# Down projection of a hybrid decoder trunk: loads of two Strassen operands placed behind the next chunk's, norm products moved into the second group's pairs, order at the end pinned

## The chip, the cores and the metric

The kernel runs on one core of one Trainium2 chip. The metric is the device time of one execution in microseconds (us), lower is better; a kernel is run three times and the median is given. A profile is one further execution, taken by the hardware profiler; its span runs from the first to the last recorded instruction, and the execution's own time is a little longer than its span.

## The reference

One decoder layer over 256 tokens of width 2048, with 16 meta tokens ahead, all in float32. Heads of differential attention and of chunkwise retention share one input projection and one output projection; then come a gated MLP with a causal convolution and a final RMS norm. Cut to what matters here:

```python
def conv_glu(u, w_gate, w_up, conv_w, w_down):
    g = u @ w_gate
    ...
    return (jax.nn.silu(gc) * (u @ w_up)) @ w_down          # 256x5632 @ 5632x2048

def reference(x, ...):
    ...
        h = h + y @ w_out[l]
        u = rmsnorm(h, ffn_norm[l]) * vmask
        h = h + conv_glu(u, w_gate[l], w_up[l], conv_w[l], w_down[l])

    out = rmsnorm(h, final_norm)
    return out[:, CHUNK:]
```

The change is in the product with `w_down` and in the final norm. Everything ahead of them stays as it was.

## The kernel before, in words

**Arithmetic.** TensorE multiplies a rounded form of float32. So each operand is split into a high half (ScalarE casts it, L223) and a low half (VectorE subtracts the cast from the original, L224), and each product is three matmuls, high by high, high by low and low by high (`triple`, L888 to L890). Weights come from DRAM in chunks, are split by `prep`, and are read by TensorE from the tiles `whi` and `wlo` (every fourth pair from `wx`, the last two from `end1a`/`end1b` and `end0a`/`end0b`).

**The down stage** runs from about 916.5 us to TensorE's last matmul at 1140.86. The 256 tokens are two row blocks of 128; the 2048 output columns are two groups, g = 0 and 1, of two blocks of 512 each. In each group the 44 slices of 128 along the inner dimension are used in two ways. 28 of them are joined in pairs to 14 *mixed* chunks p0 to p13, each a 2x2 block product in the manner of Strassen with seven products instead of eight. The other 16 are *plain* chunks of `w_down`, two pairs to a chunk.

A mixed chunk has four parts, each an entry in the order of work: "d", "u" and "c" with two products (6 matmuls), "t" with one (3 matmuls). A plain pair is one entry of 12 matmuls. The weights of a mixed chunk are quarters of `w_mix` and sums of them (`td`, made in DRAM during the gate/up stage), its activations also sums (`sd`, the *forms*). A matmul over 512 columns takes about 0.23 us from start to start, so "d" to "t" fill 1.36, 1.36, 1.36 and 0.68 us.

**Loads** (`load`) are issued by the sync queue (SP), in program order. For a mixed chunk these are: two quarters of `w_mix` (512 KB) into the tile `raw`, the forms (384 KB) into `fa` or `fb`, two blocks of `td` (512 KB) into `raw`, and then B11, the third quarter of `w_mix`, and T4, the first block of `td` (256 KB each), into a tile of its own, `sw`. Only part "c" reads `sw`. There are two `sw` tiles, taken in turn, five tiles for `raw`, and three places for the forms. A load into a tile waits until the tile's last reader is done, and whatever stands behind it on the queue waits with it. `ahead` loads a chunk when the current entry is within 6 entries of the chunk's first, and splits an entry 3 entries ahead.

**Side work** runs between the entries: `pump(n)` takes n steps off the list `side`. There `take` and `joined` add finished sums from PSUM to the residual rows `htok`, `squared` accumulates the sums of squares for the norm, `weighed` multiplies a block by the norm's weights `fn`, `norm` loads those weights for a group over GpSimd's queue (512 KB), and `norm_scale` multiplies them by a constant. `fn` has one buffer, so the load for group 1 waits until the four `weighed` of group 0's columns are done.

**The end.** The last six plain pairs of group 1 are *held* (HOLD): the matmuls on them come at the very end, over all six pairs for the first row block's last 512 columns (`o_01`) and for the two halves of 256 columns of the second row block (`oe0`, `oe1`). After `o_01` row block 0 is finished: the addition to `htok` (L1065), the sum of squares (L908), the reciprocal root (`last`), scaling (L1086, L1088) and output. After `oe0` and `oe1` (additions at L1076) the same is done for row block 1 (L1096 to L1099). Each engine executes its own list in order. The scheduler decides that list, except where `keep` pins an instruction to the place in which the code is written.

Of the kernel before, what the change touches and what calls it, by code (L numbers as in the profile page):

```python
# [15 lines left out]
ALU = mybir.AluOpType  # L16
AX = mybir.AxisListType
# [23 lines left out]
NW = 512  # L41
# [75 lines left out]
def trunk_kernel(ctx, tc, a, out):  # L117
# [45 lines left out]
    pairs = {}  # L163
    state = {"dma": 0, "prep": 0}

    def load(c):
        turn = (c - nw) % 5 if c >= nw else 0
        if turn == 3:
            t = pools["dn"].tile([P, D], F32, tag="sraw", name=f"raw{c}")
        elif turn == 4:  # L170
            t = big.tile([P, D], F32, tag="act1", name=f"raw{c}")
        else:
            t = wp.tile([P, D], F32, tag="raw", bufs=3, name=f"raw{c}")
        if c in mixed:
            g, p = divmod(mixed[c], NS)
            n = mixed[c]
            if not n:
                pools["fa"], pools["fb"] = [big.tile([P, 9 * P], F32R, tag="act2" + i,
                                                     name="f" + i) for i in "ab"]
            fa, fb = pools["fa"], pools["fb"]  # L180
            if n % 3 < 2:
                f6 = (fa, fb)[n % 3]
                sf = f6[:, :3 * P], f6[:, 3 * P:6 * P]
            else:
                sf = fa[:, 6 * P:], fb[:, 6 * P:]
            sw = big.tile([P, 2 * NW], F32, tag="act3" + "ab"[n % 2], name=f"sw{g}_{p}")
            w, sd, td = a["w_mix"][g, p], pools["sd"][p], pools["td"][g, p]
            keep(nc.sync.dma_start(out=t[:, :2 * NW], in_=w[:, :2 * NW]))
            if n % 3 < 2:
                keep(nc.sync.dma_start(out=f6[:, :6 * P].bitcast(F32), in_=sd))  # L190
            else:
                for i in range(2):
                    keep(nc.sync.dma_start(out=sf[i].bitcast(F32),
                                           in_=sd[:, 3 * i * P:3 * (i + 1) * P]))
            keep(nc.sync.dma_start(out=t[:, 2 * NW:], in_=td[:, NW:]))
            keep(nc.sync.dma_start(out=sw[:, :NW], in_=w[:, 2 * NW:3 * NW]))
            keep(nc.sync.dma_start(out=sw[:, NW:], in_=td[:, :NW]))
            pools["sf"][g, p] = sf
            pools["sw"][g, p] = sw
        else:  # L200
            ins = nc.sync.dma_start(out=t, in_=chunks[c])
            if c >= nw:
                keep(ins)
        raw[c] = t

    def prep(hf):
        c, s = entries[hf]
        held = len(entries) - 1 - hf
        if held < 2:
            hi, lo = [big.tile([P, 1024], F32R, tag=f"act{2 + held}{i}", name=f"end{held}{i}")  # L210
                      for i in "ab"]
        elif c >= nw and (hf - 2 * nw) % 4 == 3:
            wx = big.tile([P, 2 * 1024], F32R, tag="act0", name=f"wx{hf}")
            hi, lo = wx[:, :1024], wx[:, 1024:]
        else:
            hi = wp.tile([P, 1024], F32R, tag="whi", bufs=3, name=f"whi{hf}")
            lo = wp.tile([P, 1024], F32R, tag="wlo", bufs=3, name=f"wlo{hf}")

        pin = keep if hf >= 2 * nw + 4 else (lambda ins: ins)

        def halves(src, b, e):
            with tc.high_priority() if 8 < hf < 16 else nullcontext():
                pin(S.copy(out=hi[:, b:e], in_=src))  # L223
                pin(V.tensor_tensor(out=lo[:, b:e], in0=src, in1=hi[:, b:e].bitcast(F32),  # L224
                                    op=ALU.subtract))

        if c in mixed:
            g, p = divmod(mixed[c], NS)
            if s == "d":
                halves(raw[c][:, :2 * NW], 0, 2 * NW)  # L230
                pin(V.tensor_tensor(out=raw[c][:, :NW], in0=raw[c][:, :NW],
                                    in1=raw[c][:, 2 * NW:3 * NW], op=ALU.subtract))
            elif s == "u":
                halves(raw[c][:, 2 * NW:], 0, 2 * NW)
            elif s == "c":
                halves(pools["sw"][g, p], 0, 2 * NW)
            else:
                halves(raw[c][:, :NW], 0, NW)
        else:
            halves(raw[c][:, s * 1024:(s + 1) * 1024], 0, 1024)  # L240
        pairs[hf] = (hi, lo)
        if s in (1, PARTS[-1]):
            raw.pop(c)
# [536 lines left out]
    with ExitStack() as p2:  # L780
# [103 lines left out]
        HW = NW // 2  # L884
        LB = (NB - 1) * NW

        def triple(o, ah, al, wh, wl, start, stop):
            PE.matmul(o, ah, wh, start=start, stop=False)  # L888
            PE.matmul(o, ah, wl, start=False, stop=False)  # L889
            PE.matmul(o, al, wh, start=False, stop=stop)  # L890

# [4 lines left out]
        def forms(p, i):  # L896
            return [t[:, i * P:(i + 1) * P] for t in pools["sf"][g, p]]

        def down(o, m, b, hf, c0=0, n=NW, start=False, stop=False):
            whi, wlo = pairs[hf]  # L900
            for kk in range(2):
                ws = slice(kk * NW + c0, kk * NW + c0 + n)
                triple(o, *acts(m, KP + 2 * b + kk), whi[:, ws], wlo[:, ws],
                       start and kk == 0, stop and kk == 1)

        def square(m, b, e, slot):
            j = dn.tile([P, NW], F32, tag="t", name=f"sq{m}_{slot}")
# [3 lines left out]
        def weigh(m, b, e):  # L911
            h = htok[:, m, b:e]
            g = b // (2 * NW)
            ins = V.tensor_tensor(out=h, in0=h, in1=fns[g][:, b - g * 2 * NW:e - g * 2 * NW],
                                  op=ALU.mult)
            if not g:
                keep(ins)

        def known(m, n):
            V.tensor_reduce(out=pre[:, m:m + 1], in_=so[:, m, :n], axis=AX.X, op=ALU.add)  # L920
            V.tensor_scalar(out=pre[:, m:m + 1], in0=pre[:, m:m + 1],
                            scalar1=1.0 / D, scalar2=EPS, op0=ALU.mult, op1=ALU.add)

# [19 lines left out]
        for g in range(2):  # L943
# [58 lines left out]
            def weighed(m, n):  # L1002
                return lambda: weigh(m, n * NW, (n + 1) * NW)

            def take(m, j, bank=bank, res=res):
                def f():
                    add(res[m, j], bank[m, j])
                return f

# [3 lines left out]
            for i, (kind, x, y) in enumerate(seq):  # L1013
                ahead(e)
                if g and i >= len(seq) - HOLD:
                    held.append((y, e))
                    e += 1
                    pump(2)
                    continue
                wt = pairs[e]  # L1020
                if kind == "w":
                    for m in range(2):
                        for kk in range(2):
                            product((m, x % 2), acts(m, KP + 2 * y + kk), wt, kk * NW)
                elif y == "d":
                    product((0, 0), acts(0, 2 * x + 1), wt, NW)
                    product((0, 1), forms(x, 2), wt, 0)
                elif y == "u":
                    product(6, forms(x, 0), wt, 0)
                    product(7, forms(x, 1), wt, NW)  # L1030
                elif y == "c":
                    product(1, acts(0, 2 * x), wt, 0)
                    product((1, 0), acts(1, 2 * x + 1), wt, NW)
                else:
                    product(5, acts(1, 2 * x), wt, 0)
                pairs.pop(e)
                e += 1
                if i == last_s:
                    if g:
                        side.extend([weighed(m, n) for n in range(2) for m in range(2)])  # L1040
                        side.append(lambda: norm(1))
                    side.extend([take(0, 0), take(1, 0), *joined()])
                    if g:
                        side.append(lambda: norm_scale(1))
                        for m in range(2):
                            side.extend([squared(m, 2), weighed(m, 2)])
                        side.append(lambda: S.activation(out=root, in_=so[:, 1, 2:3],
                                                         func=AF.Sqrt))
                pump(3 if g and i > last_s else 1)
            if not g:  # L1050
                side.extend([take(0, 1), take(1, 1)] + [nop] * 6)
                for m, n in ((0, 0), (1, 0), (0, 1), (1, 1)):
                    side.extend([squared(m, n), nop, nop])
                continue
            pump(len(side))
            po = [bank[0, 1], bank[1, 1]]
            nb = NPL

            h1 = htok[:, 1, LB:]
            V.tensor_tensor(out=h1, in0=po[1], in1=h1, op=ALU.add)  # L1060
            known(0, NB - 1)
            for b, hf in held:
                down(po[0], 0, b, hf, stop=b == nb - 1)
# [6 lines left out]
            for c in range(2):  # L1070
                o = ps1.tile([P, NW], F32, tag="mm", bufs=3, name=f"oe{c}")[:, :HW]
                for i, (b, hf) in enumerate(held):
                    down(o, 1, b, hf, c * HW, HW, start=i == 0, stop=i == HOLD - 1)
                b_, e_ = LB + c * HW, LB + (c + 1) * HW
                hc = htok[:, 1, b_:e_]
                ins = V.tensor_tensor(out=hc, in0=o, in1=hc, op=ALU.add)  # L1076
# [104 lines left out]
```

## Time and profile before

| | |
|---|---|
| median of three runs | 1152.23 us (1151.5 to 1152.89) |
| the profiled execution, its own time | 1153.29 us |
| its span | 1151.5 us |
| mean granted clock of TensorE | 0.997 |
| HBM, whole span | 272.00 MB read, 34.08 MB written, 266 GB/s |
| last matmul ends | 1140.86 us |

The profile page gives each engine's busy time, the chain of work that ended last, and groups of instructions. Views of the trace are read besides: busy time in windows, the timeline of an engine (start, length, line, operation, output and inputs, and in brackets how long the engine had been idle and what ended that), and DMA loads with their time from issue to landing. The names in them leave out the number of a buffer: `sw` is the tile of any mixed chunk.

### The profile page before, as it was taken

Reading aid. Unit: us, or ns where it says so; the run is one execution under the profiler, and the core shown is the slowest. Engines: PE = TensorE matmul, PEld = TensorE weight load, DVE = VectorE, ACT = ScalarE, POOL = GpSimd, SP = SyncE. Lnnn points to the kernel's source line nnn. Section 1 sums busy time; section 2 is a strip of 40 time slices with the busy share of each in tenths; the row PEclk is TensorE's granted clock in tenths of the full one; section 3 lists DMA queues with packets and bytes.
Section 4 is the critical chain, followed back from the end, with each engine's and each line's share of the span. In section 5 each row is a group of like instructions: output and inputs, shape, how many; then the busy total and the mean of one; then the engine's idle time right before and its main releaser. Section 6 shows DMA issues by size and latency. Waiting matters only on the chain.

```text
span 1151.5 us, 20845 instructions
## 1 busy us (share of the span) xinstructions
PE 1136.4 (99%) x7955; PEld 1063.2 (92%) x7955; DVE 943.4 (82%) x1798; ACT 613.0 (53%) x1009; POOL 41.6 (4%) x94
## 2 busy tenths in 40 slices
PE   9999999999999999999999999999999999999996
PEld 7999999999999999999999999999999988888775
DVE  7898887667777769888888898888887788888986
ACT  7676665433345544454445444444444466756663
POOL 0000000000000000000100100000000000000000
PEclk9999999999999999999999999999999999999998
DMA  9644546475548775898989999989887599977982
GB/s 316 215 154 158 190 141 198 169 260 175 194 167 260 233 220 187 297 323 325 333 303 341 352 335 320 338 305 346 299 311 265 178 382 367 374 269 279 388 319 92
DMA packets 104387, 307.44 MB, mean 267 GB/s; under 512 B 44800, under 2 KB 55424, under 8 KB 79456
## 3 DMA queue, kind: packets, MB, share of 16 engines
q1 hardware_dynamic: 94672, 248.04, 61.6%
q0 software_dynamic: 9472, 57.94, 13.7%
q8 instruction: 62, 1.02, 0.3%
q14 instruction: 37, 0.30, 0.1%
q10 hardware_dynamic: 144, 0.14, 0.1%
HBM read 272.00 MB, written 34.08 MB: 266 GB/s over the span
## 4 chain that ended last, share of the span: by engine, by line
PE 94%; DMA 3%; DVE 1%; ACT 1%; issue 0%; SPq 0%; DVEq 0%; ACTq 0%
PE mm L475 14%; PE mm L464 10%; PE mm L462 10%; PE mm L463 10%; PE mm L454 7%; PE mm L455 7%; PE mm L456 7%; PE mm L477 7%; PE o L890 3%; PE o L889 3%; PE o L888 3%; PE x L889 2%; PE x L888 2%; PE x L890 2%; PE po L599 1%; DMA sw<-td 1%
## 5 line engine op out<-in xcount | busy, mean ns | idle before, releaser
L223 ACT CAST whi<-raw 128x1024 fp32r<-128x1024 f32 (+1 forms) x381 | 390.5, 1026 | 357.4 <-PE mm L463 85.0
L224 DVE TENSOR_TENSOR wlo<-raw,whi 128x1024 fp32r<-128x1024 f32 (+1 forms) x381 | 452.8, 1190 | 122.6 <-ACT whi L223 118.8
L475 PE MATMUL mm<-g,whi 128*128 128x512 f32 x352 | 124.4, 392 | 0.0
L464 PE MATMUL mm<-g,wlo 128*128 128x258 f32 x352 | 99.4, 282 | 0.0
L454 PE MATMUL mm<-x,whi 128*128 128x272 f32 (+1 forms) x344 | 99.3, 289 | 0.0
L462 PE MATMUL mm<-g,whi 128*128 128x260 f32 x352 | 99.2, 282 | 0.0
L456 PE MATMUL mm<-x,wlo 128*128 128x272 f32 (+1 forms) x344 | 99.0, 288 | 0.0
L455 PE MATMUL mm<-x,whi 128*128 128x272 f32 (+1 forms) x344 | 98.9, 288 | 0.0
L477 PE MATMUL mm<-g,wlo 128*128 128x256 f32 x352 | 98.7, 280 | 0.0
L463 PE MATMUL mm<-g,whi 128*128 128x256 f32 x352 | 97.8, 278 | 0.0
L475 PEld LDWEIGHTS mm<-g,whi 128*128 128x128 f32 x352 | 66.1, 188 | 13.0
L462 PE MATMUL mm<-ys,whi 128*128 128x260 f32 x256 | 71.9, 282 | 0.0
L464 PE MATMUL mm<-ys,wlo 128*128 128x258 f32 x256 | 71.8, 281 | 0.0
L463 PE MATMUL mm<-ys,whi 128*128 128x256 f32 x256 | 70.7, 276 | 0.0
L463 PEld LDWEIGHTS mm<-g,whi 128*128 128x128 f32 x352 | 66.7, 189 | 1.9
L477 PEld LDWEIGHTS mm<-g,wlo 128*128 128x128 f32 x352 | 66.2, 188 | 0.3 <-DVE wlo L224 0.3
L462 PEld LDWEIGHTS mm<-g,whi 128*128 128x128 f32 x352 | 66.1, 188 | 0.0
L464 PEld LDWEIGHTS mm<-g,wlo 128*128 128x128 f32 x352 | 66.0, 188 | 0.0
L456 PEld LDWEIGHTS mm<-x,wlo 128*128 128x128 f32 x344 | 64.9, 189 | 0.0
L455 PEld LDWEIGHTS mm<-x,whi 128*128 128x128 f32 x344 | 64.9, 189 | 0.0
L454 PEld LDWEIGHTS mm<-x,whi 128*128 128x128 f32 x344 | 64.8, 188 | 0.0
L834 ACT COPY ful<-mm 128x256 f32<-128x256 f32 x44 | 16.4, 374 | 78.2 <-PE mm L475 75.7
(429 smaller groups left out, 3151.7 us busy)
## 6 DMA issues: line engine op xcount, KB each, us to landing
raw<-in_w_in_dram SPq DMA_DIRECT2D x44, 1024.0 KB, 5.0
raw<-in_w_gate_dram SPq DMA_DIRECT2D x44, 1024.0 KB, 7.0
raw<-in_w_up_dram SPq DMA_DIRECT2D x44, 1024.0 KB, 6.5
ts<-in_w_mix_dram POOLq DMA_DIRECT2D x28, 1024.0 KB, 7.4
td<-ts POOLq DMA_DIRECT2D x28, 768.0 KB, 9.4
raw<-in_w_out_dram SPq DMA_DIRECT2D x16, 1024.0 KB, 5.3
raw<-in_w_down_dram SPq DMA_DIRECT2D x16, 1024.0 KB, 7.7
raw<-in_w_mix_dram SPq DMA_DIRECT2D x28, 512.0 KB, 7.3
```

Of the source, the lines that this page charges most:

```text
L223: pin(S.copy(out=hi[:, b:e], in_=src))
L224: pin(V.tensor_tensor(out=lo[:, b:e], in0=src, in1=hi[:, b:e].bitcast(F32), op=ALU.subtract))
L454: PE.matmul(ps[:, :n], wh, xh, start=(k == 0), stop=False)
L455: PE.matmul(ps[:, :n], wh, xl, start=False, stop=False)
L456: PE.matmul(ps[:, :n], wl, xh, start=False, stop=(k == KT - 1))
L462: PE.matmul(ps[:, :NQ + 2], wh, src.cols(k, GO - 2, GL), start=(k == 0), stop=False)
L463: PE.matmul(ps[:, 4:NQ + 2], wh, src.cols(k, GL, GW), start=False, stop=False)
L464: PE.matmul(ps[:, 2:NQ + 2], wl, src.hi(k), start=False, stop=(k == KT - 1))
L475: PE.matmul(ps, wh, src.cols(k, GO + 2, GW), start=(k == 0), stop=(k == KT - 1))
L477: PE.matmul(ps[:, :SEQ], wl, src.cols(k, GO + 2, GL), start=False, stop=False)
L888: PE.matmul(o, ah, wh, start=start, stop=False)
L889: PE.matmul(o, ah, wl, start=False, stop=False)
```

## The change

It has three parts. First, the loads of B11 and T4 are no longer issued with their chunk: they are kept in `pending` and issued behind the loads of the next chunk (mixed or plain), at the latest before part "c" is split. Second, the four `weighed` of group 0's columns, the load of group 1's norm weights and its `norm_scale` move from the end of group 1 to a list that is spread over the second group's pairs; the takes of the first two sums come after `joined`, and fewer steps are pumped at a time. Third, the order at the end is pinned by `keep`: the weighing of all blocks but the last, the reduction in `known`, the addition to `h1`, and the first matmul of each triple of `oe`.

```diff
+    pending = []
+
+    def behind():
+        while pending:
+            pending.pop(0)[1]()
...
             keep(nc.sync.dma_start(out=t[:, 2 * NW:], in_=td[:, NW:]))
-            keep(nc.sync.dma_start(out=sw[:, :NW], in_=w[:, 2 * NW:3 * NW]))
-            keep(nc.sync.dma_start(out=sw[:, NW:], in_=td[:, :NW]))
             pools["sf"][g, p] = sf
             pools["sw"][g, p] = sw
+            behind()
+
+            def fill():
+                keep(nc.sync.dma_start(out=sw[:, :NW], in_=w[:, 2 * NW:3 * NW]))
+                keep(nc.sync.dma_start(out=sw[:, NW:], in_=td[:, :NW]))
+
+            pending.append((c, fill))
         else:
             ins = nc.sync.dma_start(out=t, in_=chunks[c])
             if c >= nw:
                 keep(ins)
+                behind()
...
             elif s == "c":
+                if pending and pending[0][0] == c:
+                    behind()
                 halves(pools["sw"][g, p], 0, 2 * NW)
...
-        def triple(o, ah, al, wh, wl, start, stop):
-            PE.matmul(o, ah, wh, start=start, stop=False)
+        def triple(o, ah, al, wh, wl, start, stop, pin=lambda ins: ins):
+            pin(PE.matmul(o, ah, wh, start=start, stop=False))
...
-            if not g:
+            if b < LB:
                 keep(ins)
...
-            V.tensor_reduce(out=pre[:, m:m + 1], in_=so[:, m, :n], axis=AX.X, op=ALU.add)
+            keep(V.tensor_reduce(out=pre[:, m:m + 1], in_=so[:, m, :n], axis=AX.X, op=ALU.add))
...
                 if g and i >= len(seq) - HOLD:
                     held.append((y, e))
                     e += 1
-                    pump(2)
+                    pump(1)
...
                 if i == last_s:
+                    side.extend([*joined(), take(0, 0), take(1, 0)])
                     if g:
-                        side.extend([weighed(m, n) for n in range(2) for m in range(2)])
-                        side.append(lambda: norm(1))
-                    side.extend([take(0, 0), take(1, 0), *joined()])
-                    if g:
-                        side.append(lambda: norm_scale(1))
                         for m in range(2):
                             side.extend([squared(m, 2), weighed(m, 2)])
...
-                pump(3 if g and i > last_s else 1)
+                pump(2 if g and i > last_s else 1)
...
                 for m, n in ((0, 0), (1, 0), (0, 1), (1, 1)):
-                    side.extend([squared(m, n), nop, nop])
+                    side.extend([squared(m, n), nop, nop, weighed(m, n), nop])
+                side.extend([nop] * 12 + [lambda: norm(1)] + [nop] * 12 + [lambda: norm_scale(1)])
...
-            V.tensor_tensor(out=h1, in0=po[1], in1=h1, op=ALU.add)
+            keep(V.tensor_tensor(out=h1, in0=po[1], in1=h1, op=ALU.add))
...
-                    down(o, 1, b, hf, c * HW, HW, start=i == 0, stop=i == HOLD - 1)
+                    down(o, 1, b, hf, c * HW, HW, start=i == 0, stop=i == HOLD - 1, pin=keep)
```

The number of instructions on each engine is the same before and after. The sync queue at the start of the down stage, before (p0 and p1 of group 0; `in_w_mix_dram` is the array `w_mix`, `td_0` and `td_1` are the sums for p0 and p1):

```order
L188 DMA raw_11503<-in_w_mix_dram 128x1024
L190 DMA fa<-sd_5848 128x768
L195 DMA raw_11503<-td_0_6120 128x1024
L196 DMA sw_0_11506<-in_w_mix_dram 128x512
L197 DMA sw_0_11506<-td_0_6120 128x512
L188 DMA raw_11550<-in_w_mix_dram 128x1024
L190 DMA fb<-sd_5849 128x768
L195 DMA raw_11550<-td_1_6378 128x1024
L196 DMA sw_1_11551<-in_w_mix_dram 128x512
L197 DMA sw_1_11551<-td_1_6378 128x512
```

and after:

```order
L194 DMA raw_11503<-in_w_mix_dram 128x1024
L196 DMA fa<-sd_5848 128x768
L201 DMA raw_11503<-td_0_6120 128x1024
L194 DMA raw_11548<-in_w_mix_dram 128x1024
L196 DMA fb<-sd_5849 128x768
L201 DMA raw_11548<-td_1_6378 128x1024
L207 DMA sw_0_11506<-in_w_mix_dram 128x512
L208 DMA sw_0_11506<-td_0_6120 128x512
L212 DMA raw_11610<-in_w_down_dram 128x2048
L207 DMA sw_1_11549<-in_w_mix_dram 128x512
```

The two loads of `sw_0` moved behind the four of p1. The same queue in group 1, before, from p2's `sw` to p4's `raw`:

```order
L196 DMA sw_2_12510<-in_w_mix_dram 128x512
L197 DMA sw_2_12510<-td_2_8993 128x512
L188 DMA raw_12566<-in_w_mix_dram 128x1024
L193 DMA fa<-sd_5851 128x384
L193 DMA fb<-sd_5851 128x384
L195 DMA raw_12566<-td_3_9120 128x1024
L196 DMA sw_3_12567<-in_w_mix_dram 128x512
L197 DMA sw_3_12567<-td_3_9120 128x512
L188 DMA raw_12613<-in_w_mix_dram 128x1024
L190 DMA fa<-sd_5852 128x768
L195 DMA raw_12613<-td_4_9258 128x1024
```

and after:

```order
L194 DMA raw_12564<-in_w_mix_dram 128x1024
L199 DMA fa<-sd_5851 128x384
L199 DMA fb<-sd_5851 128x384
L201 DMA raw_12564<-td_3_9120 128x1024
L207 DMA sw_2_12508<-in_w_mix_dram 128x512
L208 DMA sw_2_12508<-td_2_8993 128x512
L194 DMA raw_12612<-in_w_mix_dram 128x1024
L196 DMA fa<-sd_5852 128x768
L201 DMA raw_12612<-td_4_9258 128x1024
L207 DMA sw_3_12565<-in_w_mix_dram 128x512
L208 DMA sw_3_12565<-td_3_9120 128x512
```

p2's `sw` moved behind p3's tile and forms, p3's `sw` behind p4's. On VectorE, the same place in group 1, before (the low halves of p2's last parts, of the plain pair `raw_12347`, whose tile p4 takes over, and of p3):

```order
L224 TENSOR_TENSOR wlo_12575<-sw_2_12510,whi_12574 128x1024
L224 TENSOR_TENSOR wlo_12582<-raw_12509,whi_12581 128x512
L224 TENSOR_TENSOR wx_12593<-raw_12347,wx_12593 128x1024
L224 TENSOR_TENSOR wlo_12603<-raw_12566,whi_12602 128x1024
L231 TENSOR_TENSOR raw_12566<-raw_12566 128x512
L224 TENSOR_TENSOR wlo_12621<-raw_12566,whi_12620 128x1024
L224 TENSOR_TENSOR wlo_12630<-sw_3_12567,whi_12629 128x1024
```

and after:

```order
L236 TENSOR_TENSOR wlo_12573<-sw_2_12508,whi_12572 128x1024
L236 TENSOR_TENSOR wlo_12580<-raw_12507,whi_12579 128x512
L928 TENSOR_TENSOR htok_11132<-htok_11132,fn_11836 128x512
L236 TENSOR_TENSOR wx_12590<-raw_12349,wx_12590 128x1024
L236 TENSOR_TENSOR wlo_12600<-raw_12564,whi_12599 128x1024
L243 TENSOR_TENSOR raw_12564<-raw_12564 128x512
L236 TENSOR_TENSOR wlo_12620<-raw_12564,whi_12619 128x1024
L236 TENSOR_TENSOR wlo_12627<-sw_3_12565,whi_12626 128x1024
```

A product with `fn` now stands ahead of the plain pair's subtraction. TensorE's end, before (the last held pair, `end0a` and `end0b`):

```order
L890 MATMUL o_01_12493<-end0a,flo 128x512
L888 MATMUL o_01_12493<-end0a,fhi 128x512
L889 MATMUL o_01_12493<-end0b,fhi 128x512
L890 MATMUL o_01_12493<-end0a,flo 128x512
L889 MATMUL oe_13317<-end0b,fhi 128x256
L890 MATMUL oe_13317<-end0a,flo 128x256
L888 MATMUL oe_13317<-end0a,fhi 128x256
L889 MATMUL oe_13317<-end0b,fhi 128x256
L890 MATMUL oe_13317<-end0a,flo 128x256
L889 MATMUL oe_13365<-end0b,fhi 128x256
L890 MATMUL oe_13365<-end0a,flo 128x256
```

and after, from the last held pair of `o_01` on:

```order
L902 MATMUL o_01_12491<-end0a,fhi 128x512
L903 MATMUL o_01_12491<-end0b,fhi 128x512
L904 MATMUL o_01_12491<-end0a,flo 128x512
L902 MATMUL oe_13317<-whi_13186,fhi 128x256
L903 MATMUL oe_13317<-wlo_13187,fhi 128x256
L904 MATMUL oe_13317<-whi_13186,flo 128x256
```

Before, the three outputs shared each held pair, so all three ended together. Now the 36 matmuls of `o_01` come first, then 36 of `oe0` (`oe_13317`) from the first held pair on, then 36 of `oe1` (`oe_13365`).

More of the change, by code (lines that the diff above doesn't have):

```diff
@@ L897, in forms, with down @@
             return [t[:, i * P:(i + 1) * P] for t in pools["sf"][g, p]]
-        def down(o, m, b, hf, c0=0, n=NW, start=False, stop=False):
+        def down(o, m, b, hf, c0=0, n=NW, start=False, stop=False, pin=lambda ins: ins):
             whi, wlo = pairs[hf]
@@ L903, in down @@
                 triple(o, *acts(m, KP + 2 * b + kk), whi[:, ws], wlo[:, ws],
-                       start and kk == 0, stop and kk == 1)
+                       start and kk == 0, stop and kk == 1, pin)
         def square(m, b, e, slot):
@@ L1003, in weighed, with take @@
                 return lambda: weigh(m, n * NW, (n + 1) * NW)
-            def take(m, j, bank=bank, res=res):
+            def take(m, j, bank=bank, res=res, left=left):
                 def f():
+                    assert not left[m, j]
                     add(res[m, j], bank[m, j])
```

## The prediction

> **What bounds the kernel now.** I read the page's totals first, then the split of the chain of waits by engine, then busy time in 10 us windows over the down stage, because everything ahead of it stays as it was.
>
> ```profile
> span 1151.5 us, 20845 instructions
> PE 1136.4 (99%) x7955; PEld 1063.2 (92%) x7955; DVE 943.4 (82%) x1798; ACT 613.0 (53%) x1009; POOL 41.6 (4%) x94
> PE 94%; DMA 3%; DVE 1%; ACT 1%; issue 0%; SPq 0%; DVEq 0%; ACTq 0%
> ```
>
> TensorE holds 94% of the chain, and no matmul is added or removed. So the time can move in two ways only: stalls between matmuls, and the work after the last one. The windows say where stalls are (columns: stretch, length, then busy time of PE, PEld, DVE, ACT, POOL, granted clock, DMA share, GB/s):
>
> ```profile
> 1040.00:1050.00 10.00, 10.00 (x46) 8.29 (x45) 9.41 (x10) 7.40 (x9) 0.00 (x0) 1.00 0.41 126
> 1050.00:1060.00 10.00, 10.00 (x46) 8.29 (x45) 8.83 (x11) 6.51 (x8) 0.00 (x0) 1.00 0.98 343
> 1060.00:1070.00 10.00, 9.75 (x42) 7.40 (x42) 8.41 (x9) 5.68 (x6) 0.00 (x0) 1.00 1.03 414
> 1070.00:1080.00 10.00, 9.90 (x44) 7.64 (x42) 8.46 (x10) 7.32 (x9) 0.00 (x0) 1.00 1.04 413
> 1080.00:1090.00 10.00, 10.00 (x46) 8.29 (x45) 9.16 (x11) 7.00 (x8) 0.00 (x0) 1.00 1.02 389
> 1090.00:1100.00 10.00, 8.94 (x39) 6.84 (x37) 7.25 (x8) 5.43 (x6) 0.00 (x0) 1.00 1.00 360
> 1100.00:1110.00 10.00, 9.79 (x44) 8.04 (x44) 8.95 (x10) 6.99 (x9) 0.00 (x0) 1.00 0.99 377
> ```
>
> A full window starts 46 matmuls. From 1060 on they start 42, 44, 46, 39 and 44: 15 short, each worth 0.227 us (10 us over the 44 that end in it), so 3.4 us of stalls in group 1. There the DMA engines are full. From 1040 to 1050 they are 41% busy: loads that belong later could run there, and those that can't are lost. Two casts show what stalls wait for (columns: start, length, engine, line, operation; in brackets the idle time before it and what ended it):
>
> ```profile
> 1070.73 1.05 ACT L223 CAST wx<-sw 128x1024 fp32r<-128x1024 f32 x1 [1.75 <-DMA sw<-td]
> 1098.26 1.04 ACT L223 CAST wx<-raw 128x1024 fp32r<-128x1024 f32 x1 [3.59 <-DMA raw<-in_w_down_dram]
> ```
>
> One waited for the second half of a sw (B11 with T4), the other for a plain chunk queued behind a sw. Putting sw later helps the second and hurts the first.
>
> **The change part by part.** *Loads, group 0.* The sync queue issues in order, so a load stands behind whatever its predecessor waits for. p_n is mixed chunk n, c its third part, the only user of sw. (A row that ends in KB and a number gives a load's size and the us from issue to landing.)
>
> ```profile
> 916.04 0.33 SPq L196 DMA_DIRECT2D sw<-in_w_mix_dram  x1
> 920.59 0.42 DVE L840 TENSOR_TENSOR flo<-ful,fhi 128x256 fp32r<-128x256 f32 x1 [0.47 <-ACT fhi L839]
> 921.09 0.33 SPq L188 DMA_DIRECT2D raw<-in_w_mix_dram  x1
> 923.00 0.59 SPq L197 DMA_DIRECT2D sw<-td  x1
> sw<-td SPq DMA_DIRECT2D x1, 256.0 KB, 7.8
> 924.98 1.05 ACT L223 CAST whi<-sw 128x1024 fp32r<-128x1024 f32 x1 [1.67 <-PE o L890]
> 930.18 0.39 PE L888 MATMUL x<-whi,fhi 128*128 128x512 f32 x1
> 930.86 0.39 PE L889 MATMUL x<-wlo,fhi 128*128 128x512 f32 x1
> 1047.32 1.22 DVE L224 TENSOR_TENSOR wx<-raw,wx 128x1024 fp32r<-128x1024 f32 x1
> ```
>
> p0's sw was issued at 916.04, ahead of p1's raw tile, which goes at 921.09, when the last low half of gate/up is out (920.59 + 0.42). Now it stands behind that tile, in the place that p1's sw had: 923.00 plus 7.8 is 930.8. The cast takes 1.05 and the subtraction 1.22, so the high half is ready at 931.9 and the low half at 933.1. TensorE wanted them at 930.18 and 930.86. The low half is later: **+2.3 us**. TensorE's order is fixed when the program is built, so what follows c in it waits too.
>
> *Loads, group 1.* The same happens around p3 and p4.
>
> ```profile
> 1041.79 0.33 SPq L196 DMA_DIRECT2D sw<-in_w_mix_dram  x1
> 1050.11 1.05 ACT L223 CAST whi<-sw 128x1024 fp32r<-128x1024 f32 x1
> 1048.57 0.33 SPq L188 DMA_DIRECT2D raw<-in_w_mix_dram  x1
> 1050.37 0.47 SPq L197 DMA_DIRECT2D sw<-td  x1
> sw<-td SPq DMA_DIRECT2D x1, 256.0 KB, 6.2
> DMA to landing us min/median/max: 3.2/6.3/9.4
> 1055.30 0.39 PE L889 MATMUL x<-wlo,fhi 128*128 128x512 f32 x1
> 1118.20 0.69 DVE L914 TENSOR_TENSOR htok<-htok,fn 128x512 f32<-128x512 f32 x1
> ```
>
> p3's sw went at 1041.79, into the idle stretch, and was cast at 1050.11. Now it waits behind p4's raw tile, which could not go before 1048.57: its buffer was freed by the subtraction at 1047.32 + 1.22. One of the moved norm products (0.69) now precedes such a subtraction, so I add 0.6. In the place of p4's sw the second half goes at 1050.97, lands 6.2 later at 1057.2, is cast by 1058.2 and subtracted by 1059.5; TensorE wanted the low half at 1055.30: **+4.2 us**. The landing time of sw loads over the stage bounds both terms: at 3.2 us they are 0 and +1.2, at 9.4 they are +3.9 and +7.4.
>
> *The rest of group 1.* From there the DMA engines stay full, so what is added to them arrives as lateness.
>
> ```profile
> 1075.35 1.05 ACT L223 CAST wx<-sw 128x1024 fp32r<-128x1024 f32 x1 [0.19 <-DMA sw<-td]
> 1077.73 0.39 PE L888 MATMUL x<-wx,fhi 128*128 128x512 f32 x1
> fn<-in_final_norm_dram POOLq DMA_DIRECT2D x2, 512.0 KB, 5.4
> ```
>
> At the 413 GB/s of the windows 512 KB take 1.3 us and the 1408 KB of a chunk's raw tile and forms 3.4. p7's sw, cast at 1075.35 the moment it landed, comes later by p8's raw and forms (3.4), by p3's sw, now out of the idle stretch (1.3), by the product (0.6) and by the second norm load, which moves here from the end (512 KB, 1.3): 6.6 in all. TensorE itself comes 4.2 later, less the 1.4 us of earlier stalls (4 and 2 matmuls) that this lateness swallows, so 2.8; and it used p7's product 1.3 after the cast was done (1077.73 less 1076.40). That leaves 6.6 − 2.8 − 1.3 = **+2.5 us**. Bounds: 0, if the transfers catch up as at 1080, where no matmul was short; 4, if none of the 1.3 counts. Against it the stalls of before, **−3.4 us**, are gone: they are inside the new ones, and the plain chunk waited for at 1098 is now loaded ahead of a sw.
>
> The Trainium skill ("DMA: Bandwidth & Descriptors", section "Issuing engines are not separate DMA queues") says that transfers issued by the scalar, sync or gpsimd engine run on the same 16 DMA engines and interleave. The windows at 1.03 of the engines agree, since nothing is left over there. If the GpSimd queue had bandwidth of its own, the 1.3 us of the norm load would drop out and this term would be +1.2.
>
> *Norm products and takes.* Four products of 0.69 us, the halving of the norm vector and the order of the takes move into VectorE's share of the windows (8.4 to 9.4 of 10 us). They come at one step a pair, half of what is pumped today at the end. Beyond the 0.6 counted I take them at nothing: while the loads are late, VectorE waits too. If that cover is gone, they cost up to 4 × 0.69 = 2.8. At the end they leave free VectorE time that TensorE didn't wait for.
>
> *The end.* TensorE's last 108 matmuls now come by output: 36 of o_01, then 36 for each half of the other row.
>
> ```profile
> 1139.28 0.39 PE L890 MATMUL o<-end0a,flo 128*128 128x512 f32 x1
> 1139.71 0.69 DVE L1065 TENSOR_TENSOR htok<-o,htok 128x512 f32<-128x512 f32 x1 [4.16 <-PE o L890]
> 1140.58 0.28 PE L890 MATMUL oe<-end0a,flo 128*128 128x256 f32 x1
> 1143.88 0.42 DVE L1076 TENSOR_TENSOR htok<-oe,htok 128x256 f32<-128x256 f32 x1
> ```
>
> Before, o_01 ended at 1139.67, 1.2 us ahead of the end of everything (1140.58 + 0.28 = 1140.86). VectorE then worked through row 0 from 1139.71 and reached the last half's addition only at 1143.88, 3.0 late. Now 72 narrow matmuls follow o_01, 8.6 us at the 0.12 between their starts, and row 0's 4.2 us on VectorE fit beside them. The addition can start 0.04 after the last matmul (as at 1139.71), so 1140.90: −2.98. Against it I set 0.25, because o_01 takes the held pairs in 1.36 us each (six matmuls), while VectorE makes their low halves in 1.22 each and runs close behind: **−2.7 us**, between −2.4 and −3.5 (row 0's output, no longer beside that of row 1, could help by some tenths). From that addition to the span's end are 7.6 us that nothing shortens.
>
> **Sum:** +2.3 + 4.2 + 2.5 − 3.4 − 2.7 = +2.9 us. The profiled execution took 1153.29 (span 1151.5), 1.06 over the median; so 1156.2 for it, and 1155.1 on the median's scale. All low ends together (0, 1.2, 0, −3.4, −3.5) give 1146.5; the high ends (3.9, 7.4, 4, −3.4, −2.4, and 2.8 of uncovered VectorE work) lie over 1160, but the first three share one supply of transfers and don't all come.
>
> **Rivals.** *Faster:* the sw loads come in time. The mechanism is the landing of p3's sw: if it is down before 1053.0 (1055.30 less cast and subtraction), 2.6 after its issue, nothing waits there, and then the norm load is the only addition to the full stretch. What is removed stays: 1152.23 − 3.4 − 2.7 = 1146.1. For it: the DMA engines are free when p4's tile is issued. Against it: the fastest sw load of the stage took 3.2.
>
> *No change:* lateness at p3 is a gift of time to the transfers, so the later stretch adds nothing and the third term is 0: +0.4, so 1152.6. For it: 4.2 us at 413 GB/s are 1.7 MB. Against it: a buffer has to be free before its load goes, and the lateness delays that too.
>
> *Slower by the clock:* a stall of 4 us is long enough to be seen by the clock.
>
> ```profile
> 1145.00:1146.00 1.00, 0.00 (x0) 0.00 (x0) 0.93 (x5) 0.22 (x1) 0.00 (x0) 0.50 1.04 422
> ```
>
> The granted clock fell to 0.50 about 4 us after the last matmul. If a gap at p3 does the same, TensorE runs at half speed for a while after; over 3.4 us that adds 1.7, so 1156.8. By the Trainium skill ("TensorE: Matmul & The Clock Gate", section "What's actually happening") one idle window of some 3.4 us halves the clock and one as long of work restores it; the row agrees with the drop, and no run here shows a stall in mid-stage that does so.
>
> That the change doesn't do what it says can be left out: the listed orders of the sync queue, VectorE and TensorE show the new places.
>
> **How the numbers follow.** Forecast 1155.1 with 0.46; no change 0.25; faster 0.18; the clock 0.11. A measurement here tells some 0.2% (2.3 us) from none, so "same" is 1149.9 to 1154.5. It gets the 0.25 and 0.03 of the forecast's lower edge: 0.28; slower 0.54, faster 0.18. The range runs from 1148.0, which leaves out most of the faster case, to 1159.5, the forecast with the first two terms nearer their upper ends; about 2 in 10 are outside.
>
> **What would show it.** Right: a gap of 2 us on TensorE near 931, with the cast of sw waiting for its DMA; one of 3 to 4 us near 1055; fewer short windows after 1090; the last addition within 0.4 us of the last matmul. Wrong: no gap at those two places, sw casts that wait for TensorE as before, or a last addition that still comes 3 us after.

## The result and the profile after

The changed kernel takes 1161.44 us (median of 6 runs, 1160.12 to 1162.64) against 1152.56 for the kernel before (6 runs of the same session). The ratio is 1.0078 with a 95% interval of 1.0065 to 1.0091: about 8.9 us slower. The prediction had "slower" as likeliest, but 1155.1 as its time and 1159.5 as the upper end of its range.

The profiled execution has a span of 1160.1, 8.6 more than before. The page's totals and the first line of the chain of waits:

```profile
span 1160.1 us, 20860 instructions
PE 1141.9 (98%) x7955; PEld 1064.9 (92%) x7955; DVE 943.7 (81%) x1798; ACT 611.8 (53%) x1009; POOL 41.7 (4%) x94
PE 90%; DMA 4%; DVE 3%; ACT 1%; SPq 1%; issue 0%; DVEq 0%; ACTq 0%
```

TensorE's share of the chain fell from 94% to 90%; DMA, VectorE and the sync queue took the difference. The windows of the down stage (columns as in the prediction) show where. Three of group 0 before:

```profile
930.00:940.00 10.00, 10.00 (x46) 8.29 (x45) 9.69 (x10) 7.02 (x9) 0.00 (x0) 1.00 1.02 412
...
950.00:960.00 10.00, 10.00 (x46) 8.28 (x45) 8.26 (x10) 6.33 (x8) 0.00 (x0) 1.00 1.03 414
960.00:970.00 10.00, 10.00 (x46) 8.29 (x45) 8.93 (x10) 7.10 (x8) 0.00 (x0) 1.00 1.00 354
```

and after, with those of group 1:

```profile
930.00:940.00 10.00, 7.97 (x33) 6.22 (x34) 8.19 (x9) 8.15 (x9) 0.00 (x0) 1.00 1.02 411
...
950.00:960.00 10.00, 9.76 (x42) 7.70 (x43) 8.97 (x10) 7.15 (x8) 0.00 (x0) 1.00 0.72 227
960.00:970.00 10.00, 9.25 (x41) 7.36 (x40) 7.58 (x8) 4.64 (x6) 0.00 (x0) 1.00 1.03 412
...
1050.00:1060.00 10.00, 10.00 (x46) 8.29 (x45) 8.36 (x10) 4.93 (x6) 0.00 (x0) 1.00 0.33 98
1060.00:1070.00 10.00, 5.79 (x16) 4.13 (x15) 4.79 (x6) 4.50 (x5) 0.00 (x0) 0.73 1.02 391
1070.00:1080.00 10.00, 10.00 (x42) 8.04 (x41) 8.94 (x11) 6.67 (x9) 0.00 (x0) 0.93 1.03 410
1080.00:1090.00 10.00, 10.00 (x45) 8.26 (x45) 9.57 (x11) 6.56 (x8) 0.53 (x1) 1.00 1.03 394
1090.00:1100.00 10.00, 10.00 (x45) 8.28 (x45) 9.49 (x10) 6.92 (x8) 0.00 (x0) 1.00 0.98 362
```

Group 0, in which no window was short before, now has a hole at 930 and smaller ones up to 1001. From 1060 to 1070 only 16 matmuls run and the granted clock is 0.73. From 1090 to 1100, where the kernel before had only 39, nothing is missing.

The single events, on ScalarE, TensorE and the sync queue (start, length, line, operation; in brackets the idle time before and what ended it):

```profile
930.70 1.04 ACT L235 CAST whi<-sw 128x1024 fp32r<-128x1024 f32 x1 [7.80 <-DMA sw<-td]
931.79 0.50 PE L902 MATMUL x<-whi,fhi 128*128 128x512 f32 x1 [1.87 <-ACT whi L235]
942.65 1.05 ACT L235 CAST wx<-sw 128x1024 fp32r<-128x1024 f32 x1 [2.52 <-DMA sw<-td]
962.92 0.50 PE L902 MATMUL x<-whi,fhi 128*128 128x512 f32 x1 [0.75 <-ACT whi L235]
1055.50 0.33 SPq L194 DMA_DIRECT2D raw<-in_w_mix_dram  x1
1057.30 0.46 SPq L208 DMA_DIRECT2D sw<-td  x1
1064.10 1.04 ACT L235 CAST whi<-sw 128x1024 fp32r<-128x1024 f32 x1 [7.69 <-DMA sw<-td]
1065.19 0.79 PE L902 MATMUL x<-whi,fhi 128*128 128x512 f32 x1 [4.21 <-ACT whi L235]
1138.28 0.50 PE L903 MATMUL o<-wlo,fhi 128*128 128x512 f32 x1 [0.67 <-DVE wlo L236]
1152.48 0.42 DVE L1088 TENSOR_TENSOR htok<-oe,htok 128x256 f32<-128x256 f32 x1 [2.63 <-PE oe L904]
```

The load issued at 1057.30, from the view of DMA loads (size, us from issue to landing):

```profile
sw<-td SPq DMA_DIRECT2D x1, 256.0 KB, 6.6
```

Both stalls that the prediction placed are there, with sw as what is waited for. A ledger comes from the starts of all matmuls in both traces. The first column counts each step that is over 0.12 us longer than the usual 0.227 (512 columns) or 0.119 (256). It leaves out the step behind most gaps, which is 0.11 longer than usual. The second column leaves out nothing: it compares the starts of matmuls with the same number in TensorE's list, before and after (7955 in both).

| place | counted steps, us | same matmul, us |
|---|---|---|
| start of the down stage | | −0.4 |
| p0 of group 0 (931.79 and 933.05) | +2.5 | +2.8 |
| rest of group 0, seven smaller gaps from 949.9 to 1001.3 | +2.7 | +3.9 |
| p3 of group 1 (1065.19) | +4.4 | +4.4 |
| slow matmuls behind it, to 1071.3 | +3.0 | +3.0 |
| gaps of before (1066.8 to 1100.3), none now | −2.3 | −3.1 |
| small steps near 1112 of before | | +0.2 |
| a held pair's low half (1138.28) | +0.8 | +0.9 |
| last addition behind the last matmul: 0.04 instead of 3.02 | −3.0 | −3.0 |
| sum | +8.1 | +8.7 |

The spans differ by 8.6; the 0.1 is rounding. The expectations below were written with counted steps (2.7 for the rest of group 0, 2.4 for the gaps of before).

### The profile page after: what moved, and what is told of

It reads as the page before. It is cut to its first block, busy times and chain, and to the rows that moved or that the text cites. A ratio compares the mean times of both kernels' runs of the same rounds, so it can differ in the third digit from the quotient of the medians.

```text
span 1160.1 us, 20860 instructions
## 1 busy us (share of the span) xinstructions
PE 1141.9 (98%) x7955; PEld 1064.9 (92%) x7955; DVE 943.7 (81%) x1798; ACT 611.8 (53%) x1009; POOL 41.7 (4%) x94
## 4 chain that ended last, share of the span: by engine, by line
PE 90%; DMA 4%; DVE 3%; ACT 1%; SPq 1%; issue 0%; DVEq 0%; ACTq 0%
PE mm L489 14%; PE mm L478 10%; PE mm L476 10%; PE mm L477 10%; PE mm L468 7%; PE mm L469 7%; PE mm L470 7%; PE mm L491 7%; PE o L902 2%; PE o L903 2%; PE o L904 2%; DMA sw<-td 2%; PE x L903 2%; PE x L902 2%; PE x L904 2%; DVE wlo L236 1%
```

## Experiments

Twelve kernels were run. Each was timed beside the kernel before on the same chip, whose median was 1152.3 to 1153.0.

**1. The loads alone** (loads_only). The kernel before with the first part of the change, its diff as shown above (`pending`, `behind`, `fill`) and nothing else.

> The kernel before with the first part alone (B11 and T4 behind the next chunk's loads). Theory, that all the loss is in this part: the stalls of the changed kernel come back, 2.5 us at p0 of group 0, 2.7 in the rest of that group, about 3.8 at p3 of group 1 (4.4 less the 0.6 of the norm product), and the 2.4 us of late stalls are gone: 1152.5 + 2.5 + 2.7 + 3.8 - 2.4 = 1159 if the clock holds over a gap of 3.8, 1162 if it falls to 0.50 for some 6 us again. Rival, that the norm products and their load cost a good part of it: under 1157.

1162.45 us, ratio 1.0086 (1.0071 to 1.0101). It has the gaps again: 2.4 at p0, 1.5 in the rest of group 0 (2.7 by the same matmul), 3.6 at p3, and the slow matmuls behind, as the theory had it for a clock that falls. All of the loss is in this part. The stall at p3 is 0.7 shorter than in the changed kernel; the norm product of 0.69 that the prediction placed ahead of p4's tile is not moved here.

**2. The loads undone** (loads_back). The changed kernel with each sw issued at once; the norm products and the pinned end stay.

```diff
             pending.append((c, fill))
+            if True:
+                behind()
```

> The changed kernel with the first part undone: B11 and T4 are issued with their own chunk again; the norm products among the pairs and the pinned end stay. Theory: the end gives its 2.4 us, the late stalls of before (2.4) are back and grow by up to 1.3 through the norm load that now runs among them: 1150 to 1152. Rival, that the norm products cost among the pairs: 1153 to 1156, with gaps on TensorE near them.

1151.9 us, ratio 0.9993 (0.9983 to 1.0002). That is in the range that the theory gave, but no measurable gain. The gaps until 1101 are no larger than those of the kernel before (1.6 us in all, against 2.3), and by the same matmul TensorE has lost nothing there by 1101 (under 0.1). So the norm products cost nothing among the pairs. The last addition comes 1.8 earlier, at 1142.05 instead of 1143.88.

**3. Two loads undone** (two_back). In place of `True` stands `(g, p) in ((0, 0), (1, 3))`.

> The changed kernel, but the loads of p0 in group 0 and of p3 in group 1, the two that come to stand behind a tile that isn't free, are issued with their own chunk. Theory: the two big stalls (2.5 and 4.4) and the slow clock (3.0) go, 1161.4 - 9.9 = 1151.5; if the late stalls vanished only because that pause let the transfers catch up, 2 to 4 of them return: up to 1155. The 2.7 us in the rest of group 0 stay if they come from each load's being late, and go (1149) if they only follow from the first stall.

1158.34 us, ratio 1.0052 (1.0037 to 1.0067): a miss. The gap at p0 is gone, and the small ones of group 0 stay (2.9 us), as the theory said. But the large stall in group 1 is still there, one chunk later. ScalarE and TensorE at p4's part c:

```profile
1065.87 1.04 ACT L237 CAST whi<-sw 128x1024 fp32r<-128x1024 f32 x1 [4.57 <-DMA sw<-td]
1066.96 0.79 PE L904 MATMUL x<-whi,fhi 128*128 128x512 f32 x1 [3.02 <-ACT whi L237]
```

p4's sw stands behind p5's tile and forms, 1408 KB, in the same burst of loads. So it isn't a matter of the one load that stands behind a blocked tile. When loads restart after a block, the first sw that has let a chunk pass is late: p3's in the changed kernel, p4's here.

**4. No idle TensorE at p3** (busy_gap). The changed kernel with matmuls by zeros in the gap, which add nothing to the sum they go to.

```diff
                 elif y == "c":
+                    if g and x == 3:
+                        for _ in range(30):
+                            keep(PE.matmul(room((0, 0))[:, :SEQ], zero, fhi[:, 0],
+                                           start=False, stop=False))
```

> The changed kernel with 30 matmuls of 256 columns by a tile of zeros, added to an open sum, placed on TensorE ahead of part c of p3 in group 1, where it stands idle for 4.4 us; 30 x 0.119 = 3.6 us. Clock theory: TensorE isn't idle long enough for the clock to fall, the granted clock stays at 1.00 from 1060 to 1075, and the 3.0 us of slow matmuls go: 1158.4. Rival, that those matmuls were slow because their operands came late: no change, 1161.4, at whatever clock.

1161.47 us, ratio 1.0078 (1.0061 to 1.0095): no change, but not for the rival's reason. The clock did hold. The added matmuls and the gaps behind them on TensorE:

```profile
1060.08 3.69 PE L1052 MATMUL o<-fhi,zero 128*128 128x256 f32 x30
...
1065.56 0.50 PE L903 MATMUL x<-wlo,fhi 128*128 128x512 f32 x1 [0.23 <-DVE wlo L236]
1069.52 0.50 PE L902 MATMUL x<-whi,fhi 128*128 128x512 f32 x1 [0.43 <-ACT whi L235]
...
1088.75 0.50 PE L902 MATMUL x<-wx,fhi 128*128 128x512 f32 x1 [0.41 <-ACT wx L235]
```

And the windows of the same kernel:

```profile
1060.00:1070.00 10.00, 8.81 (x51) 6.92 (x50) 5.69 (x7) 5.04 (x7) 0.00 (x0) 1.00 1.01 383
1070.00:1080.00 10.00, 10.00 (x45) 7.92 (x44) 9.93 (x12) 6.73 (x7) 0.00 (x0) 1.00 1.04 413
1080.00:1090.00 10.00, 9.25 (x38) 6.56 (x37) 7.57 (x9) 5.82 (x7) 0.54 (x1) 1.00 1.04 410
```

With a clock of 1.00 the slow matmuls' 3.0 us are gone, and gaps of 2.4 us in all appear between 1065 and 1091 that the changed kernel didn't have. The DMA engines are full in all three windows. By the same matmul, from ahead of the gap at p3 to behind the last of these gaps, this kernel takes 0.3 us more than the changed kernel, not 3.0 less. So the slow clock only filled time in which the loads would have been late.

**5. The end alone** (end_only). The kernel before with the third part of the change.

> The kernel before with the third part alone (order at the end pinned; loads and norm products as before). Theory: the last half's addition comes right behind the last matmul, -3.0, but o_01 now waits for the low half of a held pair (0.8 in the changed kernel), so 1152.6 - 2.2 = 1150.4. Rival, that the end gains nothing without the norm products moved, since those then stand in VectorE's list ahead of the held pairs' low halves and make them later still: 1152 to 1154, with gaps of over 1 us behind 1125.

1152.62 us, ratio 1.0000 (0.9991 to 1.0009). TensorE and VectorE:

```profile
1127.64 0.50 PE L889 MATMUL o<-wlo,fhi 128*128 128x512 f32 x1 [0.84 <-DVE wlo L224]
1131.84 0.50 PE L889 MATMUL o<-end1b,fhi 128*128 128x512 f32 x1 [1.16 <-DVE end1b L224]
1143.68 0.42 DVE L1076 TENSOR_TENSOR htok<-oe,htok 128x256 f32<-128x256 f32 x1 [2.63 <-PE oe L890]
```

The last addition waits for TensorE, as planned. But o_01, run alone, uses a pair in 1.36 us and waits 2.6 us in all for low halves that VectorE makes among the norm products, the takes and the scaling of the norm's weights. What is gained at the end is lost ahead of it: the rival was right.

**6. One load deferred** (one_moved). Only p11's sw in group 1, whose next chunk is the plain one that the kernel before waited 3.59 us for (in place of `True`: `(g, p) != (1, 11)`).

> The changed kernel with a single sw load deferred, that of p11 in group 1, so that the plain chunk needed before it goes first; all others are issued with their own chunk. Beside loads_back (1151.9), theory: the gap near 1099 (0.7 there, 1.7 in the kernel before) goes and nothing else moves: 1151.0. Rival: the gap goes to part c of p11 or p12: 1151.9.

1150.61 us, ratio 0.9988 (0.9979 to 0.9997). No gap is left near 1099. Here the plain chunk is needed ahead of part c, so this order of loads is that of use. Beside experiment 2 the intervals overlap; the gain of 0.9 us at this place is read from the traces, by the same matmul.

**7. Deferred late only** (late_moved). Group 1 from p6 on (`not (g and p >= 6)`).

> The changed kernel with the loads deferred only from p6 of group 1 on, where the DMA engines are full. Beside loads_back (1151.9), order theory: the late stalls (1.7) go as they did in the changed kernel: 1150.5. Supply theory: in the changed kernel they went because TensorE had been held up before, so here stalls come back at parts c, p6 and p7 first: 1152 to 1155.

1154.79 us, ratio 1.0022 (1.0013 to 1.0031). ScalarE and TensorE at p7's part c:

```profile
1074.49 1.04 ACT L237 CAST wx<-sw 128x1024 fp32r<-128x1024 f32 x1 [4.61 <-DMA sw<-td]
1075.59 0.50 PE L904 MATMUL x<-wx,fhi 128*128 128x512 f32 x1 [2.16 <-ACT wx L237]
```

The supply theory holds: without the pause at p3 the deferred loads stall TensorE here. The gap near 1067 stays as well (0.45), and only the one near 1099 is gone. So in the changed kernel the gaps near 1067 and 1077 went because TensorE was late already, and the one near 1099 by the order of loads.

**8. Deferred in group 0 only, from p1 on** (first_moved; `g or not p`).

> The changed kernel with the loads deferred only in group 0 and there from p1 on. Beside loads_back (1151.9), theory: the deferred loads cost their 2.7 to 2.9 us in small gaps between 940 and 1001, since each starts some 3.4 us later and the chain of tiles behind it too, and nothing in group 1: 1154.8. Rival, that those gaps came from two loads blocked elsewhere: 1151.9.

1155.19 us, ratio 1.0026 (1.0017 to 1.0035). There are 2.2 us of gaps from 943.6 to 998.4 (3.1 by the same matmul), beside none in loads_back. The first of them:

```profile
943.57 0.50 PE L904 MATMUL x<-wx,fhi 128*128 128x512 f32 x1 [0.76 <-ACT wx L237]
```

The small gaps of group 0 are a cost of their own.

**9. Four plain pairs ahead of group 1's mixed chunks,** on the changed kernel (lead_after) and on one_moved (lead_one).

```diff
-LEAD = [(4, 5), (3, HOLD + 2)]
+LEAD = [(4, 5), (4, HOLD + 2)]
```

> The changed kernel with four plain pairs ahead of group 1's mixed chunks instead of three, so that the second half of a plain chunk no longer keeps its tile until the middle of the group and the loads behind it aren't blocked. Theory, that the stall at p3 and the slow clock come from loads that can't restart before that tile is free: the 7 us there go, the idle stretch of the DMA engines near 1040 to 1055 is filled, 1154 to 1156. Rival, that a sw behind another chunk is late wherever the DMA engines are full: stalls of 3 us or more come back at later parts c, 1158 or more.

> one_moved (1150.6, all sw loads but p11's with their own chunk) with the same four plain pairs ahead. Theory: the small gaps left near 1059 to 1083 (1.2 us together) go as the loads start earlier: 1149.5. Rival: fewer plain pairs are left between the mixed chunks, so the full stretch is denser and new gaps come behind it: 1151 to 1153.

1162.27 (ratio 1.0082, 1.0068 to 1.0095) and 1153.87 (1.0014, 1.0005 to 1.0023). Both theories missed. On the second new gaps come, as its rival said, 4.0 us in all from 1083 to 1115, and the time is 0.9 above the rival's range. On the first the time is that of its rival, but the large stall comes behind idle DMA engines, not full ones. No gap of group 1 is over 0.6 us until 1089. But the next plain chunk with one pair left to do blocks the queue in its turn. The sync queue and TensorE of lead_after:

```profile
1069.59 0.42 SPq L208 DMA_DIRECT2D sw<-td  x1
1080.37 0.33 SPq L194 DMA_DIRECT2D raw<-in_w_mix_dram  x1
1090.03 0.79 PE L902 MATMUL x<-whi,fhi 128*128 128x512 f32 x1 [4.25 <-ACT whi L235]
```

And its windows:

```profile
1070.00:1080.00 10.00, 9.83 (x44) 7.69 (x43) 9.93 (x12) 7.41 (x9) 0.53 (x1) 1.00 0.55 210
1080.00:1090.00 10.00, 5.78 (x26) 4.46 (x24) 3.31 (x4) 2.04 (x3) 0.00 (x0) 0.99 0.81 276
```

No load is issued for 10.8 us, the DMA engines idle, and behind the restart stands a stall of 4.4 us at a part c, as at p3. The block and the stall moved together.

**10. Held pairs for two outputs at a time,** on one_moved (both_one), and with four plain pairs ahead too (both_lead): o_01 and oe0 by turns, then oe1.

```diff
-            for b, hf in held:
-                down(po[0], 0, b, hf, stop=b == nb - 1)
+            oe0 = ps1.tile([P, NW], F32, tag="mm", bufs=3, name="oe0")[:, :HW]
+            for i, (b, hf) in enumerate(held):
+                down(po[0], 0, b, hf, stop=b == nb - 1, pin=keep)
+                down(oe0, 1, b, hf, 0, HW, start=i == 0, stop=i == HOLD - 1, pin=keep)
...
-                o = ps1.tile([P, NW], F32, tag="mm", bufs=3, name=f"oe{c}")[:, :HW]
-                for i, (b, hf) in enumerate(held):
-                    down(o, 1, b, hf, c * HW, HW, start=i == 0, stop=i == HOLD - 1, pin=keep)
+                o = oe0
+                if c:
+                    o = ps1.tile([P, NW], F32, tag="mm", bufs=3, name="oe1")[:, :HW]
+                    for i, (b, hf) in enumerate(held):
+                        down(o, 1, b, hf, HW, HW, start=i == 0, stop=i == HOLD - 1, pin=keep)
```

> one_moved with the held pairs taken by two outputs at a time: o_01 and the first half oe0 by turns, then the second half oe1 alone. A pair then lasts 2.1 us on TensorE instead of 1.36 and VectorE's low halves (1.22 each) are no longer late. Theory: the gap of 0.83 near 1127 goes; row 0's 4.2 us on VectorE stand beside oe1's 36 matmuls of 0.119 = 4.3, so the last addition comes at most 0.5 late: 1149.8 to 1150.3. Rival: that addition is late by over 0.8, and nothing is won: 1150.6 or more.

> lead_one and both_one together: if each keeps its gain, 1148.7 to 1149.5; if either gives nothing, the better of the two.

1149.87 us, ratio 0.9976 (0.9965 to 0.9987), and with four pairs ahead 1153.3, ratio 1.0006 (0.9997 to 1.0014). The first is the fastest kernel of the study, 2.6 us below the kernel before. The second missed even "the better of the two": 4.6 us of gaps stand from 1083 to 1116. Its last addition:

```profile
1140.27 0.42 DVE L1094 TENSOR_TENSOR htok<-oe,htok 128x256 f32<-128x256 f32 x1 [0.77 <-PE oe L906]
```

VectorE waited for TensorE, so row 0's work did fit beside oe1's 36 matmuls, and no gap for a low half is left. The ratios of one_moved and both_one come from separate sessions and their intervals overlap; that the held pairs' order wins is read from the trace.

## Why the prediction was wrong

The sizes in this section are those of the second column, by the same matmul.

*p0 of group 0, +2.3:* 2.8 measured, by the steps given: the sw landed at 930.6 (forecast 930.8).

*p3 of group 1, +4.2:* 4.4. The load took 6.6 us behind the blocked tile (forecast 6.2). The high half ended the stall, not the low half: the scheduler had put four more matmuls ahead of part c, and the low half came in time while the matmuls ran slowly. So the load and its wait were right, the half that decides was not, and the close size is in part luck.

*Rest of group 1, +2.5, and the clock as a rival, +1.7:* the trace has 3.0 us of slow matmuls and no late gap. Experiment 4 shows that the two are one quantity: with the clock kept up, 2.4 us of late gaps come back and the time is the same. The step's size was nearly right. What was wrong was to set the clock apart as a case of its own; it came with the forecast stall, and it cost nothing on top.

*Before's stalls, −3.4:* 3.1. The counts in the windows include matmuls that run across an edge, two in a full window and fewer beside a stall, so 15 was a little too many. The prediction gave two reasons and both hold. The gap near 1099 (1.9) is gone in every kernel that defers p11's sw and keeps three plain pairs ahead (experiment 6), and the earlier ones (1.3) were absorbed by lateness (experiment 7).

*The end, −2.7:* −3.0 and +0.9, together −2.1. The 0.25 for the held pairs' low halves was too small, since takes stand ahead of them on VectorE. Experiment 5 shows that the gain is lost altogether if the norm products stay at the end, which the prediction had at nothing. Part two alone was not run.

**The step that failed** is the one headed *Loads, group 0*. It priced p0 alone and passed over the other 13 sw loads of that group, so it put them at nothing without a reason: the windows it rests on begin at 1040, and group 0's slack was never set against a delay of 1408 KB. They cost 3.9 us in the profile of the changed kernel, 2.7 and 2.8 in experiments 1 and 4, which have the same loads there, and 3.1 when deferred alone (experiment 8). Why the size varies is open. The waits of ScalarE from 930 to 1010 show the slack used up. Before, with all casts of sw from 930 to 1010:

```profile
ACT wx L223 <- DMA sw<-td: 0.2, 1, 0.2
```

and after (us in total, times, longest):

```profile
ACT whi L235 <- DMA sw<-td: 12.6, 5, 7.8
ACT wx L235 <- DMA sw<-td: 6.5, 3, 2.7
```

One wait of 0.2 became eight of 19.1 us, 7.8 of them at p0. Before, the 14 second halves of sw landed 0.1 to 4.5 us ahead of their cast, ten of them by less than the 3.4 us that the prediction itself gives for 1408 KB. After, 12 of the 14 landed at most 0.2 us ahead of it. That part t of a chunk is cast behind c, and so frees its tile later and sends the next loads later, fits the DMA share of 0.72 near 955, but no run separates it.

Against the forecast sum of +2.9 stand +3.9 for the rest of group 0, +0.6 for the end, +0.5 for the late term with its clock, +0.7 at p0 and p3, +0.3 for the stalls of before and −0.2 for the start and the small steps: 8.7, with 8.6 measured.

## What to carry to other kernels

Order loads by the order of first use. A load that lets another pass must have that one's transfer time as slack, and this is to be checked for every instance in the loop, not only at the two where a queue is blocked. Where a supply of transfers was the limit here, a stall, a slow clock and a late wait further on were one loss seen in three places: remove one, and look for the others before counting a gain.

## What the runs showed of the hardware that had not been expected

The granted clock fell after gaps shorter than the 4 us of the prediction. The granted clock in windows of 1 us, in lead_after behind a gap of 1.9 us at p0 (the clock fell at 932.8), and in the changed kernel behind gaps of 2.0 and 0.5 at the same place:

```profile
934.00:935.00 1.00, 1.00 (x4) 0.81 (x3) 1.00 (x1) 0.42 (x1) 0.00 (x0) 0.50 1.00 405
```

```profile
934.00:935.00 1.00, 1.00 (x6) 0.79 (x5) 0.97 (x2) 0.63 (x2) 0.00 (x0) 1.00 1.03 405
```

So of two stalls of about 2 us one was followed by half speed and the other was not. The times of the changes tell more. In each trace they stand a multiple of 3.41 us apart: 6.83 and 85.3 in the changed kernel, 3.41, 153.6 and 61.4 in lead_after. On that grid the gap of lead_after falls into one stretch of 3.41 us, and those of the changed kernel are split by a boundary at 931.4, 1.6 us ahead of it and 1.1 behind. Over the down stage of all traces, stretches at full speed with 2.04 us or more of gaps and late steps in them were followed by half speed (2.04 in lead_after, 2.24 in loads_only, 2.6 in late_moved), and those with 2.01 or less (loads_only at p0) were not. So the limit is near 2.0 of 3.41 us here, an estimate from these sums. The Trainium skill ("TensorE: Matmul & The Clock Gate", section "What's actually happening") has the clock fall after one idle window of some 3.4 us, with a window that runs freely. The grid agrees with such a window; that less than 3.4 us of idleness suffices does not follow from the sentence.

And the clock stayed at 1.00 over the gap of 4.4 us at p3 when matmuls by a tile of zeros stood in 3.7 us of it.
